# Three joints of a feed-forward layer: token forms in column parts, a second queue for the first down weights, a PSUM bank for each output half

## The chip, the cores and the metric

The kernel runs on one core of a Trainium2 chip. The metric is the device time of one execution in microseconds (us). The trace calls the engines PE (TensorE, matmuls), DVE (VectorE), ACT (ScalarE), POOL (GpSimd) and SP (SyncE, which here only starts DMAs; its queue is SPq). TensorE accumulates in PSUM, which has eight banks, each 512 fp32 columns wide on 128 partitions.

## What is computed

One layer of an encoder, for a prompt of 1024 tokens and a sample of 64, with model width 1024 and feed-forward width 2816. Ahead of the feed-forward lie three token-mixing branches, which the change does not touch. What matters here is the end:

```python
    x = x + rms_norm(merged @ w_out, g_mix_post)

    h2 = rms_norm(x, g_ffn_pre)
    up = h2 @ w_ffn_up
    up_full = jnp.concatenate([ffn_left.astype(up.dtype), up], axis=1)
    upc = causal_dwconv(up_full, ffn_dw_w)
    fg, fv = jnp.split(upc, 2, axis=-1)
    x = x + rms_norm((jax.nn.gelu(fg) * fv) @ w_ffn_down, g_ffn_post)
    return (x, k, v, u_full[:, -(CONV_WIDTH - 1):], up_full[:, -(FFN_CONV_WIDTH - 1):])
```

The last item returned, the last two rows of `up`, are the `ffn_state` outputs.

## The kernel before

All products are fp32 made of rounded parts: an operand is split (`split`, lines 99 and 100) into a high part (a cast on ACT) and a low part (a subtraction on DVE), and three products of parts are added in PSUM.

**Output projection** (1599.9 to 1700.9 us). Nine tiles of tokens, t = 0 to 8 (tile 8 is the sample). For each, 48 matmuls of `mgh`/`mgl` against the resident weights `woh`/`wol` into two banks (L1397 to L1400), 24 for each half e of the output columns. `finish` takes the tile's mean square (ACT, L1307), scales and adds the residual (DVE, L1312 and L1313, the sum kept in `xr` and stored to `d_x1`), takes the second mean square (L1316) and scales again into `tt` (L1318). Tiles are gathered in groups {0, 1}, {2, 3}, {4}, {5, 6}, {7}, {8}. `turn_group` queues eight pieces for each group: piece k transposes 128 features of the group's tokens on PE (L1330, tile `h2T<first tile>_<k>`) and an ACT copy with a gain puts them into `mf` (L1332). The pieces are taken from the list `turns` between the matmuls by `turn_some`, which keeps an estimated time `now` and lets a piece go every `gap`. After a group's last piece its list in `THEN` goes to `others`, which `turn_some` hands out every `rest`. So the program order on each engine is fixed by these estimates, when the program is written; nothing is reordered on the chip.

**Feed-forward up** (to 2194 us). For each of 22 feature blocks f, gate and value together are one 2 x 2 block product that is made with seven products j = 0 to 6 in place of eight. Each takes a sum or difference of token quarters (`X[g][j]`, tiles `xa<j>h`, `xa<j>l` for token columns up to 548, group A; `xb<j>h`, `xb<j>l` for group B) and one of weight blocks (`wf<j>`, made by `w_form` from the loaded `gw`, `vw`). A product of one group is 12 matmuls of 274 columns (L1452 to L1454) into a bank of `ff<f>_<j><g>`. Sums of token quarters are made in place by `sub` (L1237), the temporary ones in `wsl` and `wsh`, later in rows of `mf`. Group A's forms come from `forms_a`, whole (4 x 274 = 1096 columns at a time), after the group {4}. Group B's sums are made in three parts after {5, 6}, {7} and {8}; its forms are split whole once all transposes are done, ahead of block 0's products for group B. Block 0 runs its seven products for group A, with the last tiles' transposes between, then the seven for group B; from block 1 on a product serves both groups. The weight forms run five products ahead (`AHEAD`); those of block 1 are all made after the last product of block 0. Behind a product come the three-tap convolution (L1492, L1494), gelu (L1507), gate times value (L1511) and the store to `d_gu` (L1512).

**Down projection** (2208.5 us to the end). `wd_load` loads 128 rows of the weights (`wdr`, L1553) and splits them into `wd<f>h`, `wd<f>l`; `g_load` loads gate-value columns from `d_gu` (L1564, `g_0r`, `g_384r` and so on) and splits them. All loads stand on SP, in program order. Tiles 0 to 2 run together, f by f, each of their matmuls 512 columns wide (L1582, L1583, L1585). The other six tiles run one by one, the features in chunks of 6, 6, 6 and 4, in each chunk first all of output half 0, then all of half 1. After the last chunk of a half `close_half` takes the mean square (ACT, L1600; a copy on L1597 and a sum on L1598 go ahead of it for the sample) and multiplies by the gain (DVE, L1601) into `fo`. `y_banks` takes one tile of two banks from the pool `ff`, which feed-forward up used before, and gives each half one of them. Between the stages two transposes (`flT`) turn the last two rows for the `ffn_state` outputs.

## Time and profile before

| | us |
|---|---|
| median of 3 runs | 2488.18 |
| lowest, highest | 2487.49, 2489.12 |
| profiled execution, its time | 2489.66 |
| span of that profile | 2487.9 |
| TensorE busy in the span | 2409.8 (97%) |

The span reaches from the first to the last instruction of the profile; the execution's own time has 1.76 us more. All moments below count from the span's start. A row of a timeline has the start, the duration, the engine, the line, the operation, the names output<-inputs without their numbers, and in brackets the idle time of the engine just before and what ended it. Matmuls are pipelined: one that lasts 0.29 us can be followed by the next after 0.13. In a row of windows each engine has its busy time and, in brackets, its instructions; the last three numbers are the granted clock of TensorE as a share of full speed, the busy share of the DMA engines and GB/s.

### The profile page before, as it was taken

Reading aid. Unit: us, or ns where it says so; the run is one execution under the profiler, and the core shown is the slowest. Engines: PE = TensorE matmul, PEld = TensorE weight load, DVE = VectorE, ACT = ScalarE, POOL = GpSimd, SP = SyncE. Lnnn points to the kernel's source line nnn. Section 1 sums busy time; section 2 is a strip of 40 time slices with the busy share of each in tenths; the row PEclk is TensorE's granted clock in tenths of the full one; section 3 lists DMA queues with packets and bytes.
Section 4 is the critical chain, followed back from the end, with each engine's and each line's share of the span. In section 5 each row is a group of like instructions: output and inputs, shape, how many; then the busy total and the mean of one; then the engine's idle time right before and its main releaser. Section 6 shows DMA issues by size and latency. Waiting matters only on the chain.

```text
span 2487.9 us, 37659 instructions
## 1 busy us (share of the span) xinstructions
PE 2409.8 (97%) x15167; PEld 2280.5 (92%) x15167; DVE 1703.2 (68%) x2081; ACT 1055.2 (42%) x1965; POOL 103.4 (4%) x263
## 2 busy tenths in 40 slices
PE   8999999999999999999989999998999999979998
PEld 6999999999899998999889999986999999968776
DVE  6687878888665887787887436338988888853221
ACT  7324242424555666666664203145433333333111
POOL 2000000000000000000000000011101111100000
PEclk9999999999999999999999999998999999989999
DMA  7222222121555332433353546122222222155331
GB/s 266 89 66 87 75 67 93 62 93 62 155 158 135 86 89 74 100 90 92 95 162 124 196 139 203 59 94 68 79 79 79 79 70 78 46 160 160 101 95 41
DMA packets 287183, 257.74 MB, mean 104 GB/s; under 512 B 63407, under 2 KB 255555, under 8 KB 287009
## 3 DMA queue, kind: packets, MB, share of 16 engines
q1 hardware_dynamic: 287009, 255.34, 34.1%
q8 instruction: 119, 1.95, 0.3%
q14 instruction: 55, 0.45, 0.1%
HBM read 165.47 MB, written 68.19 MB: 94 GB/s over the span
## 4 chain that ended last, share of the span: by engine, by line
PE 54%; DVE 5%; issue 3%; ACT 2%; DMA 1%; POOL 1%; SPq 0%; ACTq 0%; DVEq 0%; POOLq 0%
PE ff L1452 6%; PE ff L1454 6%; PE ff L1453 6%; PE dn L1582 4%; PE dn L1583 4%; PE dn L1585 3%; PE aT L859 1%; PE cv L158 1%; PE sb L158 1%; PE sb L157 1%; PE cv L157 1%; PE cv L156 1%; PE sb L156 1%; DVE r L808 1%; PE av L878 1%
## 5 line engine op out<-in xcount | busy, mean ns | idle before, releaser
L423 DVE SCALAR_TENSOR_TENSOR acc<-u,cw,acc 128x1118 f32<-128x1118 f32 x240 | 331.6, 1382 | 5.6
L99 ACT CAST whi<-wraw 128x1024 fp32r<-128x1024 f32 x112 | 118.1, 1054 | 294.3 <-PE cv L157 73.1
L808 DVE TENSOR_TENSOR_SCAN r<-r 128x128 f32<-128x128 f32 (+7 forms) x128 | 173.3, 1355 | 65.4 <-ACT r L804 64.8
L156 PE MATMUL g<-hh,whi 128*128 128x362 f32 (+1 forms) x576 | 190.6, 331 | 0.0
L158 PE MATMUL g<-hh,wlo 128*128 128x362 f32 (+1 forms) x576 | 189.9, 330 | 0.0
L157 PE MATMUL g<-hl,whi 128*128 128x362 f32 (+1 forms) x576 | 189.8, 330 | 0.0
L100 DVE TENSOR_TENSOR wlo<-wraw,whi 128x1024 fp32r<-128x1024 f32 x112 | 136.5, 1220 | 35.3 <-ACT whi L99 35.2
L1464 DVE TENSOR_TENSOR mf<-mf,ff 128x548 f32<-128x548 f32 (+1 forms) x161 | 110.3, 697 | 57.8 <-PE ff L1454 57.6
L1494 DVE SCALAR_TENSOR_TENSOR mf<-mf,fw 128x1090 f32<-128x1090 f32 x88 | 118.9, 1351 | 16.0 <-ACT mf L1492 15.3
L100 DVE TENSOR_TENSOR atl<-aT,ath 128x512 fp32r<-128x512 f32 (+1 forms) x160 | 98.4, 631 | 26.4 <-ACT ath L99 25.4
L99 ACT CAST ath<-aT 128x512 fp32r<-128x512 f32 (+1 forms) x160 | 85.4, 550 | 68.0 <-PE aT L859 58.7
L803 ACT ACTIVATE be<-z 128x128 f32<-128x128 f32 (+2 forms) x192 | 95.6, 498 | 36.1 <-PE z L832 20.9
L156 PEld LDWEIGHTS g<-hh,whi 128*128 128x128 f32 x576 | 108.9, 189 | 0.1
L157 PEld LDWEIGHTS g<-hl,whi 128*128 128x128 f32 x576 | 108.5, 188 | 0.2
L158 PEld LDWEIGHTS g<-hh,wlo 128*128 128x128 f32 x576 | 108.4, 188 | 0.0
L809 DVE TENSOR_TENSOR be<-be,r 128x127 f32<-128x127 f32 (+7 forms) x128 | 96.6, 755 | 3.0
L804 ACT ACTIVATE r<-z 128x128 f32<-128x128 f32 (+2 forms) x192 | 95.8, 499 | 0.1
L877 PE MATMUL av<-ath,vp 128*128 128x256 f32 x320 | 82.2, 283 | 1.7 <-DVE os L884 1.3
L878 PE MATMUL av<-atl,vp 128*128 128x256 f32 x320 | 78.8, 285 | 1.9 <-DVE atl L100 1.9
L544 ACT ACTIVATE gt<-g 128x362 f32<-128x362 f32 (+1 forms) x72 | 33.8, 470 | 84.8 <-PE g L158 83.4
L830 PE MATMUL z<-ks,qd 128*128 128x256 f32 (+2 forms) x192 | 69.8, 365 | 0.0
L156 PE MATMUL v<-hh,whi 128*128 128x384 f32 (+1 forms) x192 | 69.4, 361 | 0.0
(1441 smaller groups left out, 7856.2 us busy)
## 6 DMA issues: line engine op xcount, KB each, us to landing
wraw<-in_w_in SPq DMA_DIRECT2D x72, 512.0 KB, 3.9
d_gate<-gt SPq DMA_DIRECT2D x24, 544.0 KB, 4.2
d_gu<-mf SPq DMA_DIRECT2D x22, 545.0 KB, 3.1
vw<-in_w_ffn_up SPq DMA_DIRECT2D x22, 512.0 KB, 3.7
gw<-in_w_ffn_up SPq DMA_DIRECT2D x22, 512.0 KB, 3.9
wdr<-in_w_ffn_down SPq DMA_DIRECT2D x22, 512.0 KB, 4.7
wraw<-in_w_mem_kv SPq DMA_DIRECT2D x16, 512.0 KB, 5.1
qd<-qd SPq DMA_DIRECT2D x24, 272.0 KB, 4.1
```

Of the source, the lines that this page charges most:

```text
L99: ACT.copy(out=hi, in_=src)
L100: DVE.tensor_tensor(out=lo, in0=src, in1=hi.bitcast(F32), op=ALU.subtract)
L156: PE.matmul(ps, wh[:, k, :], rh[k][c], start=first, stop=False)
L157: PE.matmul(ps, wh[:, k, :], rl[k][c], start=False, stop=False)
L158: PE.matmul(ps, wl[:, k, :], rh[k][c], start=False, stop=last)
L423: DVE.scalar_tensor_tensor(out=acc, in0=u[:, t : t + 1118], scalar=cw[:, t * 8 + i : t * 8 + i + 1], in1=acc, op0=ALU.mult, op1=ALU.add,)
L808: DVE.tensor_tensor_scan(out=rv, data0=rv, data1=rv, initial=1.0, op0=ALU.mult, op1=ALU.min)
L1452: PE.matmul(ps, w[:, k, :], xh[:, k, :], start=k == 0, stop=False)
L1453: PE.matmul(ps, w[:, k, :], xl[:, k, :], start=False, stop=False)
L1454: PE.matmul(ps, w[:, 4 + k, :], xh[:, k, :], start=False, stop=k == 3)
L1464: DVE.tensor_tensor(out=out, in0=a, in1=ps, op=ALU.add)
L1494: DVE.scalar_tensor_tensor(out=acc, in0=raw[:, t : NO + t], scalar=fw[:, t * 44 + m : t * 44 + m + 1], in1=acc, op0=ALU.mult, op1=ALU.add,)
```

## The change

There are five parts.

1. `forms_a` is replaced by `sums(g, j0, j1)`, which makes sums and splits for columns j0 to j1 of a quarter. Group A's are made in columns 0 to 238 after the group {2, 3} and in 238 to 274 after {4}. `turn_some` lets a piece go every 0.6 in place of 1.2 estimated us, and a queued form every 1.2 in place of 1.6.
2. Group B's splits are made in the same three column parts as its sums (74, 128, 72). They are kept and written out after the last piece, ahead of the second half of block 0; what of them can run earlier does so as the engines reach them.
3. Block 1's weight forms are made one by one behind products 1 to 5 of the second half of block 0.
4. `wdr0`, `wdr1` and the first gate-value tile are loaded by DMAs that ACT starts. The copy of `flT` goes to rows of `mf` that are free and stands, with the two state stores, ahead of the last store to `d_gu`. On SP the load of the gain `gfpost`, which stood behind the loads for features 2 to 6, comes right behind that store, ahead of the second gate-value tile.
5. The pool `ff` is closed after feed-forward up, and the down projection takes each output half from a pool `yp` of eight tiles of one bank.

```diff
-    def turn_some(dt, gap=1.2, rest=1.6):
+    def turn_some(dt, gap=0.6, rest=1.2):
...
-    def forms_a():
-
-        q11, q12, q21, q22 = quarters(0)
+    def tiles_a():
         X[0] = x_tiles(
...
+    def sums(g, j0, j1):
+
+        if g == 0 and X[0] is None:
+            tiles_a()
+        t2, t3 = (w[:, : 4 * NG].rearrange("p (k t) -> p k t", k=4) for w in ws) if g == 0 else (T2, T3)
+        q11, q12, q21, q22, t2, t3 = (q[:, :, j0:j1] for q in quarters(g) + [t2, t3])
 
         def form(j, src):
-            return lambda: split(*X[0][j], src)
-
-        return [
-            lambda: sub(t3, q22, q12), form(0, q11), lambda: sub(q12, q12, q11), lambda: sub(t2, q22, q12), form(1, t2),
-            form(2, t3), form(3, q12), form(4, q22), form(5, q21), lambda: sub(q21, q21, t2), form(6, q21),
+            return lambda: split(*(x[:, :, j0:j1] for x in X[g][j]), src)
+
+        return [lambda: sub(t3, q22, q12), lambda: sub(q12, q12, q11), lambda: sub(t2, q22, q12)], [
+            form(0, q11), form(1, t2), form(2, t3), form(3, q12), form(4, q22), form(5, q21),
+            lambda: sub(q21, q21, t2), form(6, q21),
         ]
...
+    PART = TP // 2 - NG
+    kept = []
 
     def sums_b(j0, j1):
-        q11, q12, q21, q22, t2, t3 = (q[:, :, j0:j1] for q in quarters(1) + [T2, T3])
-        return [lambda: sub(t3, q22, q12), lambda: sub(q12, q12, q11), lambda: sub(t2, q22, q12)]
-
-    LAST = (0, TP - 128 - 548 - NG, TP - 548 - NG, NG)
-    THEN = {4: forms_a, 5: lambda: sums_b(0, LAST[1]), 7: lambda: sums_b(*LAST[1:3]), 8: lambda: sums_b(*LAST[2:])}
+        first, then = sums(1, j0, j1)
+        kept.append(then)
+        return first
+
+    def sums_a(j0, j1):
+        first, then = sums(0, j0, j1)
+        return first[:1] + then[:1] + first[1:] + then[1:]
+
+    THEN = {
+        2: lambda: sums_a(0, PART), 4: lambda: sums_a(PART, NG),
+        5: lambda: sums_b(*LAST[0:2]), 7: lambda: sums_b(*LAST[1:3]), 8: lambda: sums_b(*LAST[2:4]),
+    }
...
-    ff = ctx.enter_context(tc.tile_pool(name="ff", bufs=4, space=PSUM, reuse_waits="tile"))
+    ff = banks.enter_context(tc.tile_pool(name="ff", bufs=4, space=PSUM, reuse_waits="tile"))
...
-    X[1] = x_tiles(lambda j, e: bp.tile([P, 4, NG], F32R, name=f"xb{j}{e}"))
-    q11, t1, q21, q22 = quarters(1)
-    for j, src in enumerate((q11, T2, T3, t1, q22, q21, q21)):
-        if j == 6:
-            sub(q21, q21, T2)
-        split(*X[1][j], src)
+    assert len(kept) == 3
+    for fs in kept:
+        for f in fs:
+            f()
     AHEAD = 5
     for j in range(7):
         product(0, j, (1,))
-        for n in range(AHEAD) if j == 6 else ():
-            w_form(1, n)
+        if 0 < j <= AHEAD:
+            w_form(1, j - 1)
...
+    fo = mf[:88, 7, 256 : 256 + 2 * P]
+    ACT.copy(out=fo, in_=tp[:88, : 2 * P])
+    for a, nm in enumerate(("ffn_state_prompt", "ffn_state_sample")):
+        SP.dma_start(out=O[nm][0, 0].rearrange("r (f c) -> (r f) c", c=P), in_=fo[:, a * P : (a + 1) * P])
     held.close()
+    banks.close()
+    yp = ctx.enter_context(tc.tile_pool(name="yp", bufs=8, space=PSUM, reuse_waits="tile"))
...
-            SP.dma_start(out=raw, in_=I["w_ffn_down"][0][f * P : (f + 1) * P, :])
+            (ACT if f < 2 else SP).dma_start(out=raw, in_=I["w_ffn_down"][0][f * P : (f + 1) * P, :])
...
-        SP.dma_start(
+        (ACT if f0 == t0 == 0 else SP).dma_start(
             out=raw.rearrange("p (f t) -> p f t", f=nf),
...
     def y_banks(t):
-        both = ff.tile([P, 2, 512], F32, tag="ff", name=f"dn{t}", bufs=4)
-        return [both[:, e, :] for e in range(2)]
+        return [yp.tile([P, 512], F32, tag="y", name=f"dn{t}_{e}", bufs=8) for e in range(2)]
```

What this does to the order of instructions is shown at three places. In these rows a name ends with a running number of its tile, and the brackets name the counters that the instruction waits for.

ScalarE beside output tile 6, before (`h2T2_k` and `h2T4_k` are transposed pieces of tiles 2, 3 and of tile 4, `tt5` the squares of tile 5, `mgh7` the next tile's high part):

```order
L1307 ACTIVATE tt5_16631,oms5_16632<-y5_0_16550 128x512 [waits PE_49,Pool_49]
L1332 ACTIVATE mf_14602<-h2T2_5_16595,vec_91 128x256 [waits PE_49]
L1332 ACTIVATE mf_14602<-h2T2_6_16605,vec_91 128x256 [waits PE_49]
L1332 ACTIVATE mf_14602<-h2T2_7_16615,vec_91 128x256 [waits PE_49]
L1332 ACTIVATE mf_14602<-h2T4_0_16625,vec_91 128x128 [waits PE_49]
L99 CAST mgh7_16649<-mf_14602 128x1024 [waits PE_49]
L1307 ACTIVATE tt5_16631,oms5_16632<-y5_1_16551 128x512 [waits PE_49]
L1332 ACTIVATE mf_14602<-h2T4_1_16660,vec_91 128x128 [waits PE_49]
L1332 ACTIVATE mf_14602<-h2T4_2_16669,vec_91 128x128 [waits PE_49]
L1332 ACTIVATE mf_14602<-h2T4_3_16678,vec_91 128x128 [waits PE_49]
```

The same place now:

```order
L1307 ACTIVATE tt5_16643,oms5_16644<-y5_0_16554 128x512 [waits PE_49,Pool_49]
L99 CAST xa1h_16452<-wsh_16464 128x4x238 [waits DVE_49]
L1332 ACTIVATE mf_14602<-h2T4_0_16632,vec_91 128x128 [waits PE_49]
L1332 ACTIVATE mf_14602<-h2T4_1_16638,vec_91 128x128 [waits PE_49]
L99 CAST xa2h_16454<-wsl_16465 128x4x238
L1307 ACTIVATE tt5_16643,oms5_16644<-y5_1_16555 128x512
L99 CAST mgh7_16661<-mf_14602 128x1024
L1332 ACTIVATE mf_14602<-h2T4_2_16672,vec_91 128x128 [waits PE_49]
L1332 ACTIVATE mf_14602<-h2T4_3_16678,vec_91 128x128 [waits PE_49]
```

The cast of group A's form 1 (`xa1h`, from the sum `wsh` that VectorE makes) stands ahead of the copies of tile 4's first two pieces, and further casts lie between the others.

VectorE ahead of block 0's products for group B, before (`xb0l` is the low part of group B's first form; the rows of 4 x 128 and 4 x 72 columns on L1237 are sums of token quarters, L1464 adds a product):

```order
L100 TENSOR_TENSOR xb0l_17128<-mf_14602,xb0h_17127 128x1096
L1464 TENSOR_TENSOR mf_14602<-mf_14602,ff0_40_17049 128x274 [waits DVE_49,PE_49]
L1237 TENSOR_TENSOR mf_14602<-mf_14602 128x4x128 [waits Activation_49]
L100 TENSOR_TENSOR xb5l_17138<-mf_14602,xb5h_17137 128x1096
L1237 TENSOR_TENSOR mf_14602<-mf_14602 128x4x128 [waits DVE_49]
L1464 TENSOR_TENSOR mf_14602<-mf_14602,ff0_50_17070 128x274 [waits PE_49]
L1237 TENSOR_TENSOR mf_14602<-mf_14602 128x4x128 [waits DVE_49]
L1464 TENSOR_TENSOR mf_14602<-mf_14602,ff0_60_17089 128x274 [waits PE_49]
L1237 TENSOR_TENSOR mf_14602<-mf_14602 128x4x72 [waits Activation_49]
```

The last rows ahead of the same form's last part now:

```order
L1237 TENSOR_TENSOR mf_14602<-mf_14602 128x4x72 [waits Activation_49]
L100 TENSOR_TENSOR xb1l_16994<-mf_14602,xb1h_16993 128x4x128 [waits Activation_49]
L1237 TENSOR_TENSOR mf_14602<-mf_14602 128x4x72 [waits DVE_49]
L100 TENSOR_TENSOR xb3l_16998<-mf_14602,xb3h_16997 128x4x128
L1237 TENSOR_TENSOR mf_14602<-mf_14602 128x4x72 [waits DVE_49]
L100 TENSOR_TENSOR xb4l_17000<-mf_14602,xb4h_16999 128x4x128
L100 TENSOR_TENSOR xb5l_17002<-mf_14602,xb5h_17001 128x4x128
L100 TENSOR_TENSOR xb0l_16992<-mf_14602,xb0h_16991 128x4x72
```

The low part of form 0 for the last 72 columns stands behind three sums of 72 and the splits of 128 columns of forms 1, 3, 4 and 5. In before form 0 was split whole, ahead of the sums of the last parts, which do not touch it.

TensorE where tile 3 of the down projection goes from output half 0 to half 1, in the last chunk, before (`dn3` holds both halves, `wd18h` and `g18_384h` are high parts of weights and gate-value):

```order
L1582 MATMUL dn3_22505<-wd21h_22374,g18_384h_22592 128x512
L1583 MATMUL dn3_22505<-wd21l_22375,g18_384h_22592 128x512
L1585 MATMUL dn3_22505<-wd21h_22374,g18_384l_22593 128x512
L1582 MATMUL dn3_22505<-wd18h_22296,g18_384h_22592 128x512 [waits DVE_49]
L1583 MATMUL dn3_22505<-wd18l_22297,g18_384h_22592 128x512
L1585 MATMUL dn3_22505<-wd18h_22296,g18_384l_22593 128x512
```

And now (`dn3_0` and `dn3_1` are the halves):

```order
L1601 MATMUL dn3_0_22559<-wd21h_22428,g18_384h_22647 128x512
L1602 MATMUL dn3_0_22559<-wd21l_22429,g18_384h_22647 128x512
L1604 MATMUL dn3_0_22559<-wd21h_22428,g18_384l_22648 128x512
L1601 MATMUL dn3_1_22560<-wd18h_22350,g18_384h_22647 128x512
L1602 MATMUL dn3_1_22560<-wd18l_22351,g18_384h_22647 128x512
L1604 MATMUL dn3_1_22560<-wd18h_22350,g18_384l_22648 128x512
```

The first matmul of half 1 waited for VectorE and carries no wait now. The other five tiles that run one by one show the same.

## Rows read from the trace of the kernel before

**Rows 1.** The page, busy time, share of the span and instructions of TensorE

```profile
PE 2409.8 (97%) x15167; PEld 2280.5 (92%) x15167; DVE 1703.2 (68%) x2081; ACT 1055.2 (42%) x1965; POOL 103.4 (4%) x263
```

**Rows 2.** Windows: busy us (instructions) of each engine, granted clock, DMA

```profile
1599.90:1700.90 101.00, 101.00 (x469) 82.26 (x468) 47.85 (x51) 44.26 (x91) 17.28 (x39) 1.00 0.21 71
1700.90:1727.50 26.60, 18.97 (x105) 16.85 (x104) 21.82 (x35) 16.42 (x38) 3.19 (x7) 0.74 0.37 109
1727.50:1747.00 19.50, 14.74 (x95) 14.21 (x95) 17.22 (x26) 10.93 (x16) 2.08 (x6) 0.82 0.00 1
1747.00:2194.00 447.00, 447.00 (x3520) 447.00 (x3519) 374.00 (x474) 171.35 (x226) 49.33 (x126) 1.00 0.22 72
2194.00:2208.50 14.50, 0.44 (x5) 0.18 (x3) 7.78 (x8) 4.45 (x5) 0.00 (x0) 0.59 0.48 156
2221.00:2300.00 79.00, 79.00 (x351) 65.40 (x350) 30.90 (x29) 26.00 (x30) 0.00 (x0) 1.00 0.57 171
2300.00:2487.90 187.90, 172.46 (x753) 140.47 (x751) 43.02 (x52) 28.92 (x59) 9.06 (x18) 1.00 0.27 78
```

**Rows 3.** Timeline of TensorE, 1700 to 1750: start, us, what, [idle before]

```profile
1703.39 0.39 PE L1452 MATMUL ff<-xa0h,wf 128*128 128x274 f32 x1 [2.31 <-ACT mf L1332]
...
1709.41 0.59 PE L1452 MATMUL ff<-xa1h,wf 128*128 128x274 f32 x1 [2.70 <-ACT wf L99]
...
1712.46 0.60 PE L1454 MATMUL ff<-xa1h,wf 128*128 128x274 f32 x1 [2.23 <-DVE wf L100]
...
1732.43 0.60 PE L1452 MATMUL ff<-xb1h,wf 128*128 128x274 f32 x1 [3.14 <-ACT xb1h L99]
...
1734.65 0.60 PE L1453 MATMUL ff<-xb1l,wf 128*128 128x274 f32 x1 [1.62 <-DVE xb1l L100]
...
1745.76 0.29 PE L1452 MATMUL ff<-xa0h,wf 128*128 128x274 f32 x1
```

**Rows 4.** Groups of VectorE by form, 1599.9 to 1750: busy, mean ns

```profile
L1237 DVE TENSOR_TENSOR wsh<-mf 128x1096 f32<-128x1096 f32 x1 | 1.3, 1296 | 0.0
...
L1237 DVE TENSOR_TENSOR mf<-mf 128x288 f32<-128x288 f32 x3 | 1.4, 456 | 1.0 <-ACT mf L1332 1.0
...
L100 DVE TENSOR_TENSOR wf<-gw,wf 128x512 fp32r<-128x512 f32 x4 | 2.7, 682 | 0.0
```

**Rows 5.** Timeline of VectorE, 1663 to 1673

```profile
1664.84 0.75 DVE L1318 TENSOR_SCALAR tt<-xr,or 128x1024 f32<-128x1024 f32 x1 [2.24 <-POOL or L198]
```

**Rows 6.** Timelines of ScalarE, SP's queue and TensorE, 2193 to 2216

```profile
2195.29 1.21 ACT L1492 ACTIVATE mf<-mf,fw 128x1090 f32<-128x1090 f32 x1 [2.06 <-DVE mf L1464]
2196.56 1.12 ACT L1507 ACTIVATE mf<-mf 128x1090 f32<-128x1090 f32 x1
...
2200.70 0.32 SPq L1512 DMA_DIRECT2D d_gu<-mf  x1
2201.12 0.37 SPq L1553 DMA_DIRECT2D wdr<-in_w_ffn_down  x1
2201.59 0.82 SPq L1564 DMA_DIRECT2D g_0r<-d_gu  x1
...
2205.81 1.05 ACT L99 CAST wd0h<-wdr 128x1024 fp32r<-128x1024 f32 x1 [7.88 <-DMA wdr<-in_w_ffn_down]
2207.60 0.83 ACT L99 CAST g_0h<-g_0r 128x768 fp32r<-128x768 f32 x1 [0.75 <-DMA g_0r<-d_gu]
...
2208.49 0.79 PE L1582 MATMUL dn<-wd0h,g_0h 128*128 128x512 f32 x1 [14.06 <-ACT g_0h L99]
...
2215.16 0.39 PE L1582 MATMUL dn<-wd1h,g_0h 128*128 128x512 f32 x1
```

**Rows 7.** DMA engines from 2190 to 2201.5

```profile
DMA packets 2, 0.02 MB, mean 2 GB/s; under 512 B 0, under 2 KB 0, under 8 KB 0
```

**Rows 8.** TensorE waits, 2290 to 2488: total, times, longest; one place

```profile
PE dn L1582 <- DVE fo L1601: 7.8, 5, 1.6
PE dn L1582 <- DVE fo L1598: 1.4, 1, 1.4
...
2327.83 0.39 PE L1585 MATMUL dn<-wd21h,g_384l 128*128 128x512 f32 x1
...
2329.72 0.50 PE L1582 MATMUL dn<-wd18h,g_384h 128*128 128x512 f32 x1 [1.50 <-DVE fo L1601]
```

More of the change, by code (lines that the diff above doesn't have):

```diff
@@ L1517, in encoder_step @@
     w_load(1)
+    X[1] = x_tiles(lambda j, e: bp.tile([P, 4, NG], F32R, name=f"xb{j}{e}"))
     for j in range(7):
@@ L1631, in encoder_step @@
     junk = gp.tile([P, 512], BF16, name="junk")
-    fo = gp.tile([88, 2 * P], F32, name="flo")
-    ACT.copy(out=fo, in_=tp[:88, : 2 * P])
-    for a, nm in enumerate(("ffn_state_prompt", "ffn_state_sample")):
-        SP.dma_start(out=O[nm][0, 0].rearrange("r (f c) -> (r f) c", c=P), in_=fo[:, a * P : (a + 1) * P])
     ys = {t: y_banks(t) for t in first}
```

2 lines of the change are left out of this document (1 added, 1 removed).

## The prediction

> **What bounds the kernel now.** I read the page's busy shares first, then the mean clock and busy time by stage, then TensorE's own rows in the stages where it is not full, and last what it waited for there. TensorE is busy 97% of the span [rows 1], so only a stage where it is not full has something to give. By stage [rows 2] it is full in the output projection (101.00 of 101.00 us), in the feed-forward from the second feature block on (447.00 of 447.00) and in the down projection's first part (79.00 of 79.00). It is not full at three joints, and those are what the change touches.
>
> Joint 1, from 1700.9 (last product of the output projection) to 1745.76 (first matmul of feature block 1) [rows 2, 3]: 44.86 us. The work in it is 14 products of 12 matmuls. 3520 matmuls in 447.00 us [rows 2] is 0.127 us each, so 14 x 12 x 0.127 = 21.3 us. Some sixteen transposes of the last token tiles come on top; no row has one alone, so I bound one between 0.06 us (0.127 x 128/274, by columns) and 0.25, take 0.14, and have 2.3 us (1.0 to 4.0). So 23.6 us is work and 21.3 us is loss. Of that loss 2.31 + 2.70 + 2.23 + 3.14 + 1.62 = 12.0 us are five waits that name their releasers [rows 3]: the copy of a transpose, the weight forms, the halves of group B's token forms. The other 9.3 us is clock: the two stretches ran at 0.74 and 0.82 of full [rows 2], between the levels 1.2 and 2.4 GHz, and a matmul takes 0.60 us there against 0.29 [rows 3].
>
> Joint 2, 2194 to 2208.5: TensorE busy 0.44 of 14.50 us [rows 2]. The first down matmul waited 14.06 us for the cast of the first gate tile [rows 6]. Behind it is a chain: the last gate-value store leaves SP at 2200.70, and only behind it in SP's queue go the first down weights (2201.12) and the first gate tile (2201.59), which neither need nor touch that store's data.
>
> Joint 3, the rest of the down projection: 172.46 of 187.90 busy [rows 2]. Of this, six waits of TensorE for VectorE, 7.8 + 1.4 = 9.2 us [rows 8], are of one kind: the second output half's first matmul of the last feature chunk waits until VectorE has read the first half. Both halves are one tile of two banks.
>
> **The change part by part.**
>
> *Own bank for each half.* It removes those six waits: the second half's matmul carries no wait now. Price of one: the last matmul of half 0 starts at 2327.83, the next would start 0.23 later (2328.06), it starts at 2329.72 [rows 8]: 1.66 us, and about 0.1 us more because it lasts 0.50 and not 0.39. With 5 x 1.75 for the longer kind and 1.64 for the other: 10.4 us (at least 9.2, by the waits alone). What is late next there? ScalarE's and VectorE's pass over half 0 now lies beside 12 matmuls of half 1 (2.8 us), against 1.4 us that it takes. The clock stays 1.00 in this stage, so nothing else comes back. The tail after the last matmul is what it was. I take 10.4, range 9.2 to 10.8.
>
> *Down weights and first gate tile on ScalarE's queue.* They no longer stand behind the store. ScalarE is free for them after the last gelu (2196.56 + 1.12 = 2197.68); the copy of the state rows is moved ahead of the gelu, into 2.06 us that ScalarE waits there anyway [rows 6], so it costs nothing as long as that wait stands, else its 0.35 us. So the weights go at about 2197.75 in place of 2201.12, the gate tile at about 2198.2 in place of 2201.59. From issue to cast the gate tile took 2207.60 - 2201.59 = 6.0 us and the cast 0.83 [rows 6]: 2198.2 + 6.0 + 0.83 = 2205.0, against 2208.49. No load leaves ScalarE's queue in the trace of before; SP's issues here last 0.32 to 0.82 us [rows 6]. If each of the two ahead takes 0.82, the start is 2206.2 and the gain 2.3; if the gate tile lands in the 4.7 us of the weights, 2203.7 and 4.8. Less than nothing would need a ScalarE that is held past 2201.12, and nothing stands on it then. Moved along: the two small state stores now go ahead of the last gate-value store, when SP is idle; the 0.5 MB gain load now stands on SP ahead of the second gate tile. ScalarE casts in order, so the second weights' cast stands behind that second gate tile: issued near 2201.6, landing some 6 us later, cast by 2208.4, the weights' halves by 2210.7, and feature block 1 needs them 2215.16 - 2208.49 = 6.7 us after the first matmul [rows 6], at 2211.7. Margin 1.0 us; beyond it, each us late is a us of TensorE. I take 3.5 us (1.3 to 4.8, the lower end with a us of such lateness).
>
> Here a rule speaks against the change. The rows show the loads held 3.4 us by an unrelated wait at the head of SP's queue [rows 6]. The Trainium skill (DMA: Bandwidth & Descriptors, section "Issuing engines are not separate DMA queues") says that loads started on several engines run on the same 16 DMA engines and save only the sequencer's time to initiate them. By it the part would be worth some 0.8 us, the sum 15.3 and the time 2472.9. In this place what is saved is a wait at the queue's head, which the rule does not speak of; no run here shows a load on ScalarE's queue.
>
> *Token forms.* Group A's forms are made in 238 and 36 columns, the first part already beside output tiles 5 and 6; group B's in 74, 128 and 72 columns beside the first half of block 0; block 1's weight forms go among the second half's products. The work is the same number of elements and some 30 more instructions; VectorE (47.85 of 101.00 us) and ScalarE (44.26) have room in total [rows 2]. The order in which they stand decides. I followed the four engines' queues through joint 1 with the trace's duration of each kind; [rows 4] has the three that the lines below use (a pass of 952 columns, by 1.30 us for 1096, is 1.13, and 1.2 with its start).
>
> - Tile 6: VectorE comes free of tile 4 at 1664.84 + 0.75 [rows 5] and then runs four passes of 1.2 and a small one: the sum that ScalarE's cast of form 1 needs is ready at about 1670.8. Behind that cast stand the copies of transposes 4_0 and 4_1 on ScalarE, and transposes 4_2 and later need their two banks. TensorE, which waited for nothing here, waits 1.7 + 1.3 us, with 0.35 in tiles 3 and 5: 3.35 us. A bound below is 0, if the sums run earlier.
> - Tile 8: ScalarE's first weight cast waits for a load that itself waits for a store of tile 6's rows; transpose 5_3 stands behind it: 1.54 us. Block 0 then begins after the last copy of group {5, 6}: 1.45 us, where the wait was 2.31.
> - First half of block 0: 1.55 (a copy late in ScalarE's order), 1.77 (transpose 7_2 behind a weight cast) and 0.5: 3.8 us, against 2.70 + 2.23 and slow clock.
> - Second half: its second matmul needs form 0's low part for the last 72 columns. After the last copy stand on VectorE three sums of 72 columns (0.46 each), four splits of 128 (0.68 each) and then this split (0.46): 4.6 us, against 3.14 + 1.62. I add 2.5 us of half-speed matmuls behind it.
>
> The loss is 3.35 + 1.54 + 1.45 + 3.8 + 4.6 + 2.5 = 17.2 us, in place of 21.3: a gain of 4.1 us; block 1 would start at about 1741.7. From block 1 on TensorE found every form ready and I find no new wait.
>
> *Sum.* 10.4 + 3.5 + 4.1 = 18.0 us. The profiled execution took 2489.66 us, its span 2487.9 plus 1.76 around it; less 18.0 that is 2471.7. The median of the three runs, 2488.18, is 1.5 below the profiled execution, so 2470.2.
>
> **The rivals.**
>
> *Joint 1 as meant* (0.27): sums and casts run early enough that tiles 3 to 8 stay full, and the clock stays up through block 0. For it: 53 us of VectorE's and 57 us of ScalarE's time in the output projection are free [rows 2]. Against: in-order queues at the places above. Without the first two lines and the added slow clock, 17.2 - 4.9 - 2.5 = 9.8 us of loss remain, so joint 1 gives 11.5, the sum is 25.4 and the time 2462.8.
>
> *Joint 1 gives nothing* (0.20): the stalls of tile 6 and of the first half each bring TensorE to the lower level, as the waits of 2 to 3 us did in before. Two more such half-speed stretches cost 2.5 us each: joint 1 loses 0.9, the sum is 13.0 and the time 2475.2.
>
> *Slower* (0.02): the wait of tile 6 recurs in each of the groups {4}, {5, 6}, {7} and {8}, each time at 2.5 us and with the whole clock loss of joint 1 as it was in before (9.3 us), 11.8 together: 47 us in place of 21.3, 26 us more against 13.9 from the other joints: 2500. It decides from 35.2 us of loss in joint 1 on, three recurrences. Against it: these groups' copies are spread over 12 us each.
>
> *The bank split does nothing* (0.03): if the second half is held by something that ends as late as VectorE's read, joint 3 gives 0: sum 7.6, time 2480.6. Against: the chain has nothing else there.
>
> *Only issue time is saved at joint 2* (0.05), the mechanism in which the loads, though issued earlier, land little earlier, because they wait for the same transfers: then only the issues ahead of the gate tile are saved, 0.32 for the store and 0.47 for the weights [rows 6], 0.8 us in place of 3.5. Sum 15.3, time 2472.9. Against: the DMA engines moved 0.02 MB in the 11.5 us up to the store [rows 7].
>
> **How the numbers follow.** The forecast has 0.43, its own range 2467 to 2473. About 0.2% (5 us) is what a measurement of this kernel can tell from no change. Leaving out a tenth at either end, the range is 2461 to 2479. Faster by over 0.2% means below 2483.2: all cases but the slower one and part of the split's, 0.95; within it 0.03; slower 0.02.
>
> **What would show it.** Right: no wait of `dn` matmuls for the line that reads half 0, and a stage of 177.5 us where it was 187.9; the first weights issued on ScalarE's queue within 0.3 us of the gelu's end and the first `dn` matmul near 3.5 us earlier after the last feed-forward matmul; transposes of tile 4 waiting on ScalarE in tile 6, and a wait of 4 to 5 us at the second matmul of block 0's second half. Wrong: output tiles with no wait at all and block 1 starting 33 us after the last output matmul (joint 1 as meant), or granted clock under 1.00 between tiles 5 and 8 (nothing gained there).

## The result and the profile after

The changed kernel takes 2474.55 us (median of 4 runs, 2470.70 to 2475.29) against 2487.91 for the kernel before on the same chip (median of 4). The ratio is 0.9942, 95% interval 0.9925 to 0.9960: about 13.4 us faster, with 18.0 forecast. The profiled execution took 2475.29 us, its span is 2473.5.

To see where the time went, I read a few moments from TensorE's timeline in each profile and took the lengths between them. "Joint 1" here runs from the first matmul of the output projection to the first of feature block 1, so that it also holds what the output tiles lose. "Joint 2" is from the last feed-forward matmul to the first matmul of down block 2, "blocks 2 to 21" from there to the first matmul of tile 3, "joint 3" from there to the last matmul of all.

| us | before | after | difference | forecast |
|---|---|---|---|---|
| joint 1 | 145.87 | 143.86 | -2.0 | -4.1 |
| rest of the feed-forward | 448.15 | 448.15 | 0 | 0 |
| joint 2 | 25.34 | 23.83 | -1.5 | -3.5 |
| blocks 2 to 21 | 81.60 | 81.85 | +0.25 | 0 |
| joint 3 | 180.39 | 169.32 | -11.1 | -10.4 |
| tail | 6.66 | 6.69 | 0 | 0 |

The differences give 14.3 of the 14.4 us by which the spans differ; the rest lies ahead of joint 1. Joint 3 came as forecast; each of the other two gave about half.

TensorE's share on the page is 97% again (busy time 2408.1 us, as in [rows 1] within 2 us): the work is the same, less of the span is empty. The windows by stage, with the columns of [rows 2] (span and busy time of each engine with its instructions, then granted clock, DMA share and GB/s), of the changed kernel:

```profile
1599.90:1705.30 105.40, 101.87 (x473) 82.16 (x471) 55.43 (x71) 48.24 (x106) 17.45 (x40) 1.00 0.20 71
1705.30:1743.60 38.30, 29.54 (x185) 27.43 (x185) 33.39 (x67) 23.48 (x58) 4.78 (x12) 0.87 0.24 68
1743.60:2191.90 448.30, 448.30 (x3530) 448.30 (x3530) 374.47 (x474) 172.46 (x227) 49.76 (x126) 1.00 0.22 72
2191.90:2200.20 8.30, 0.42 (x4) 0.17 (x2) 7.30 (x7) 4.50 (x5) 0.00 (x0) 0.80 0.60 196
2200.20:2215.60 15.40, 12.22 (x36) 8.86 (x37) 4.62 (x5) 3.49 (x4) 0.00 (x0) 0.78 0.78 243
2215.60:2297.40 81.80, 81.80 (x361) 67.44 (x361) 34.56 (x33) 29.81 (x38) 1.00 (x3) 1.00 0.56 171
2297.40:2473.50 176.10, 169.79 (x750) 140.25 (x748) 41.18 (x50) 26.62 (x53) 10.23 (x16) 0.99 0.29 84
```

What to see: the output projection, full in [rows 2], is 105.40 long and 3.5 us of it are empty. The empty stretch ahead of the first down matmul shrank from 14.50 to 8.30. But the first two down blocks that follow, full once they had begun in before, have 3.2 us of waits (their granted clock is 0.78; over the same two blocks of before it was 0.76).

TensorE's timeline in joint 1 (start, length, instruction, idle time before it and what ended it), changed kernel, answering to [rows 3]:

```profile
1671.16 0.33 PE L1330 MATMUL h2T<-ident,tt 128*128 128x128 f32 x1 [1.13 <-ACT mf L1332]
...
1674.09 0.33 PE L1330 MATMUL h2T<-ident,tt 128*128 128x128 f32 x1 [1.09 <-ACT mf L1332]
...
1698.30 0.44 PE L1330 MATMUL h2T<-ident,tt 128*128 128x128 f32 x2 [1.22 <-ACT mf L1332]
...
1706.30 0.40 PE L1466 MATMUL ff<-xa0h,wf 128*128 128x274 f32 x1 [0.82 <-ACT mf L1332]
...
1711.59 0.39 PE L1466 MATMUL ff<-xa2h,wf 128*128 128x274 f32 x1 [1.73 <-ACT mf L1482]
...
1713.83 0.33 PE L1330 MATMUL h2T<-ident,tt 128*128 128x128 f32 x1 [1.21 <-ACT mf L1332]
...
1730.52 0.60 PE L1467 MATMUL ff<-xb0l,wf 128*128 128x274 f32 x1 [4.37 <-DVE xb0l L100]
...
1743.66 0.29 PE L1466 MATMUL ff<-xa0h,wf 128*128 128x274 f32 x1
```

The waits for weight forms of [rows 3] are gone. In their place stand those that the orders of ScalarE and VectorE named: the two of tile 4's transposes in output tile 6, one in tile 8, two in the first half of block 0, and the long one at the second matmul of its second half. At the start of block 0 a wait of 0.82 us stands where it was 2.31.

Joint 2, rows of ScalarE, of the two DMA queues (ACTq, SPq) and of TensorE, answering to [rows 6]:

```profile
2194.46 1.11 ACT L1521 ACTIVATE mf<-mf 128x1090 f32<-128x1090 f32 x1
2194.46 0.39 ACTq L1572 DMA_DIRECT2D wdr<-in_w_ffn_down  x1
2194.89 0.44 ACTq L1583 DMA_DIRECT2D g_0r<-d_gu  x1
...
2198.35 1.04 ACT L99 CAST wd0h<-wdr 128x1024 fp32r<-128x1024 f32 x1 [2.78 <-DMA wdr<-in_w_ffn_down]
2199.33 0.83 ACT L99 CAST g_0h<-g_0r 128x768 fp32r<-128x768 f32 x1
...
2198.60 0.35 SPq L1526 DMA_DIRECT2D d_gu<-mf  x1
2199.04 0.38 SPq L1656 DMA_DIRECT2D gfpost<-in_g_ffn_post  x1
2199.51 0.79 SPq L1583 DMA_DIRECT2D g_0r<-d_gu  x1
...
2206.97 0.83 ACT L99 CAST g_0h<-g_0r 128x768 fp32r<-128x768 f32 x1 [6.80 <-DMA g_0r<-d_gu]
2207.70 1.04 ACT L99 CAST wd1h<-wdr 128x1024 fp32r<-128x1024 f32 x1
...
2200.22 0.80 PE L1601 MATMUL dn<-wd0h,g_0h 128*128 128x512 f32 x1 [7.89 <-ACT g_0h L99]
...
2208.80 0.50 PE L1601 MATMUL dn<-wd1h,g_0h 128*128 128x512 f32 x1 [2.33 <-ACT wd1h L99]
2210.06 0.50 PE L1602 MATMUL dn<-wd1l,g_0h 128*128 128x512 f32 x1 [0.76 <-DVE wd1l L100]
```

The first down matmul comes 8.41 us after the last feed-forward matmul (2191.81), where it was 14.58: a gain of 6.2, more than the 3.5 forecast. It does not last. The second weights' cast (`wd1h`) stands on ScalarE behind the second gate tile's. That tile's load was issued on SP behind the store and the 0.5 MB gain load, and its cast began 7.5 us later. ScalarE idled 6.80 us in front of it, and TensorE then waited 2.33 + 0.76 us at block 1.

Joint 3: in [rows 8] six waits, 9.2 us; from 2215 us on the changed kernel's TensorE has no wait at all. The place of [rows 8] where tile 3 goes from half 0 to half 1, now 0.23 us from one matmul to the next:

```profile
2324.46 0.39 PE L1604 MATMUL dn<-wd21h,g_384l 128*128 128x512 f32 x1
2324.69 0.39 PE L1601 MATMUL dn<-wd18h,g_384h 128*128 128x512 f32 x1
```

### The profile page after: what moved, and what is told of

Its sections match the earlier page's. It is cut to its first block, busy times and chain, and to the rows that moved or that the text cites. A ratio compares the mean times of both kernels' runs of the same rounds, so it can differ in the third digit from the quotient of the medians.

```text
span 2473.5 us, 37712 instructions
## 1 busy us (share of the span) xinstructions
PE 2408.1 (97%) x15167; PEld 2279.3 (92%) x15167; DVE 1705.1 (69%) x2108; ACT 1055.2 (43%) x1986; POOL 105.6 (4%) x263
## 4 chain that ended last, share of the span: by engine, by line
PE 54%; DVE 5%; ACT 2%; issue 2%; DMA 1%; POOL 1%; SPq 0%; DVEq 0%; POOLq 0%; ACTq 0%
PE ff L1466 6%; PE ff L1467 6%; PE ff L1468 6%; PE dn L1602 4%; PE dn L1601 4%; PE dn L1604 3%; PE aT L859 1%; DVE r L808 1%; PE cv L158 1%; PE sb L158 1%; PE sb L157 1%; PE cv L157 1%; PE cv L156 1%; PE sb L156 1%; PE av L878 1%
## 5 line engine op out<-in xcount | busy, mean ns | idle before, releaser
L1508 DVE SCALAR_TENSOR_TENSOR mf<-mf,fw 128x1090 f32<-128x1090 f32 x88 | 118.9, 1352 | 16.8 <-ACT mf L1506 16.1
```

The source lines that it names most:

```text
L1508: DVE.scalar_tensor_tensor(out=acc, in0=raw[:, t : NO + t], scalar=fw[:, t * 44 + m : t * 44 + m + 1], in1=acc, op0=ALU.mult, op1=ALU.add,)
```

## The experiments

Eleven variants and the kernel before again. The table has the lengths as above, in us, for each profile; the text below says what was changed. The last column is the median time, with the kernel before at 2487.0 to 2489.4 beside them.

| kernel | joint 1 | joint 2 | blocks 2 to 21 | joint 3 | time |
|---|---|---|---|---|---|
| before | 145.87 | 25.34 | 81.60 | 180.39 | 2487.91 |
| before again | 145.27 | 25.87 | 81.60 | 180.37 | 2487.93 |
| banks only | 144.27 | 25.04 | 83.15 | 169.32 | 2478.98 |
| queue only | 143.90 | 18.64 | 84.32 | 180.42 | 2484.77 |
| forms only | 143.71 | 24.57 | 81.60 | 180.40 | 2486.21 |
| after | 143.86 | 23.83 | 81.85 | 169.32 | 2474.55 |
| second gate tile on ScalarE's queue | 143.97 | 18.57 | 83.82 | 169.32 | 2471.58 |
| the same, three raw buffers | 142.38 | 18.74 | 86.27 | 169.32 | 2471.12 |
| splits by form | 139.20 | 22.02 | 83.68 | 169.32 | 2469.16 |
| old pace | 139.75 | 23.98 | 82.17 | 169.32 | 2469.10 |
| group A whole | 144.27 | 22.01 | 85.01 | 169.32 | 2475.73 |
| three mends | 139.31 | 19.04 | 81.60 | 169.32 | 2465.15 |
| three mends, slow pace | 135.90 | 18.85 | 81.60 | 169.31 | 2461.52 |
| three mends, middle pace | 136.72 | 18.88 | 81.60 | 169.32 | 2462.51 |

**One part at a time.** First theory: the three joints are separate, and the parts add up.

Banks only, on the kernel before:

```diff
-    ff = ctx.enter_context(tc.tile_pool(name="ff", bufs=4, space=PSUM, reuse_waits="tile"))
+    ff = banks.enter_context(tc.tile_pool(name="ff", bufs=4, space=PSUM, reuse_waits="tile"))
...
     held.close()
+    banks.close()
+    yp = ctx.enter_context(tc.tile_pool(name="yp", bufs=8, space=PSUM, reuse_waits="tile"))
...
-        both = ff.tile([P, 2, 512], F32, tag="ff", name=f"dn{t}", bufs=4)
-        return [both[:, e, :] for e in range(2)]
+        return [yp.tile([P, 512], F32, tag="y", name=f"dn{t}_{e}", bufs=8) for e in range(2)]
...
```

> The kernel before with the bank of its own for each output half alone (and what it needs: the state copy and its stores go ahead of the last gate-value store, and the feed-forward's pool is closed). Theory, joints are separate and the six waits are all of joint 3: the down projection's one-by-one part is 10.4 to 11.1 us shorter, the joints ahead of it stay as in the kernel before, time 2476.8 to 2477.6. Rival, part of the changed kernel's 11.1 us at that joint comes from its earlier start or its other loads: under 9.2 us, time above 2478.7.

Measured 2478.98 us (2475.71 to 2481.34; ratio 0.9958, 0.9943 to 0.9973), just above the rival's bound of 2478.7. But joint 3 itself is 169.32 in this kernel, 11.1 us shorter, to the hundredth the length it has in the changed kernel. Of that, 1.55 us came back in blocks 2 to 21: TensorE's timeline there has two waits at block 16, for a gate tile's cast and for its low part, which the kernel before does not have:

```profile
2275.88 0.50 PE L1588 MATMUL dn<-wd16h,g_0h 128*128 128x512 f32 x1 [0.30 <-ACT g_0h L99]
2277.28 0.50 PE L1591 MATMUL dn<-wd16h,g_0l 128*128 128x512 f32 x1 [0.66 <-DVE g_0l L100]
```

So the six waits are all of joint 3 and worth 11.1 us. That the gate tiles come late is another matter, taken up below.

Queue only, on the kernel before:

```diff
-            SP.dma_start(out=raw, in_=I["w_ffn_down"][0][f * P : (f + 1) * P, :])
+            (ACT if f < 2 else SP).dma_start(out=raw, in_=I["w_ffn_down"][0][f * P : (f + 1) * P, :])
...
-        SP.dma_start(
+        (ACT if f0 == t0 == 0 else SP).dma_start(
```

> The kernel before with the first two down weights and the first gate tile loaded from ScalarE's queue, alone. Here the order on ScalarE puts the second weights' cast ahead of the second gate tile's, and on SP the gain load still stands ahead of the second gate tile. Theory, in the changed kernel the block-1 wait of 2.3 + 0.8 us comes from the order of the two casts on ScalarE: no such wait here, the first down matmul 6 us earlier than before and block 2 some 5 to 6 us earlier, time 2482 to 2483. Rival, the loads from two queues share the DMA engines and the second weights land late whatever the order: a wait of 2 to 3 us at block 1 again, a gain of 1.5, time 2486.4.

Measured 2484.77 us (2483.87 to 2488.51; ratio 0.9987, 0.9977 to 0.9996), 4 us less than before on that chip (2488.88), where the theory had 2482 to 2483. Joint 2 went from 25.34 to 18.64, 6.7 us, with no wait at block 1; then blocks 2 to 21 took 2.7 us more, which the theory did not have. Rows of ScalarE, SP's queue and TensorE show both, in the queue-only kernel:

```profile
2201.57 1.05 ACT L99 CAST wd1h<-wdr 128x1024 fp32r<-128x1024 f32 x1 [0.27 <-DMA wdr<-in_w_ffn_down]
2207.59 0.83 ACT L99 CAST g_0h<-g_0r 128x768 fp32r<-128x768 f32 x1 [4.97 <-DMA g_0r<-d_gu]
...
2243.60 0.38 SPq L1564 DMA_DIRECT2D g_0r<-d_gu  x1
...
2259.40 1.05 ACT L99 CAST wd18h<-wdr 128x1024 fp32r<-128x1024 f32 x1 [2.81 <-DMA wdr<-in_w_ffn_down]
2260.35 0.83 ACT L99 CAST g_0h<-g_0r 128x768 fp32r<-128x768 f32 x1
...
2261.23 0.50 PE L1582 MATMUL dn<-wd14h,g_0h 128*128 128x512 f32 x1 [0.50 <-ACT g_0h L99]
2262.62 0.50 PE L1585 MATMUL dn<-wd14h,g_0l 128*128 128x512 f32 x1 [0.66 <-DVE g_0l L100]
```

Here the second weights are cast as soon as they land, at 2201.57, and the late gate tile stands behind them and is in time for block 2. The order of the two casts was the cause of the block-1 wait, not a late load of the weights. The second group of rows is the giving back: at block 14 TensorE waits for a gate tile whose cast stands behind that of weights 18, which are needed four blocks later and were waiting for their load. The gate tile's own load had been issued at 2243.60, 16.8 us ahead of its cast, while the gate tiles of joint 2 took at most 7.5 from issue to cast.

Forms only is the changed kernel with the loads, banks and state stores of before:

> The kernel before with the token forms' column parts, the faster pace of the transposes and block 1's weight forms moved, alone; loads and banks as before. Theory, the joints add up: block 1 starts 2.1 us earlier as in the changed kernel, with the same waits (tile 6 two of 1.1, block 0's second half 4.4), time 2485.8. Rival, the shared profile hides more (the forecast's 4.1): 2483.8.

Measured 2486.21 us (2482.89 to 2487.85; ratio 0.9988, 0.9978 to 0.9998). Joint 1 is 143.71, with the same waits (1.13, 1.10, 1.75, 4.37). The theory fits; but what to compare it with is in doubt, since the two other kernels, in which every engine's instructions up to block 1 stand in the order of before, show 144.27 and 143.90 and not 145.87. To answer that, the kernel before was run once more, unchanged:

> The kernel before once more, for a second profile of its first joint. In its profile block 1 starts 145.9 us after the first output matmul; in the kernels that change only the banks or only the queue, with the same code up to there, 144.3 and 143.9. Theory, the stretches at the lower clock fall differently from execution to execution, and the joint takes 144 to 146 us here too: then the changed kernel's gain there is between 0 and 2 us. Rival, 145.9 is fixed for this kernel and something in the other two shortens it: 145.7 to 146.1 again.

It took 2487.93 us (one run), and joint 1 was 145.27: not the 145.87 that the rival called fixed. The same 16 us of the program, from 104.11 us after the first output matmul, in the two executions of the kernel before, first the one of [rows 2 and 3], then this one (columns as above; the clock is the third number from the end):

```profile
1704.00:1720.00 16.00, 11.06 (x54) 10.41 (x55) 12.98 (x21) 10.49 (x22) 2.40 (x5) 0.57 0.38 105
```

```profile
1702.37:1718.37 16.00, 10.36 (x65) 9.81 (x66) 13.80 (x24) 10.85 (x23) 2.39 (x5) 0.79 0.39 103
```

One execution passed 54 instructions at 0.57 and the other 65 at 0.79, with the same waits but for one (2.70 and 3.41 us for the weight form). Two stretches tell the four executions of this joint apart. Granted clock, with the stretch counted from the first output matmul:

| kernel | 104.1 to 120.1 us | 131.5 to 139.0 us | joint 1, us |
|---|---|---|---|
| before | 0.57 | 0.56 | 145.87 |
| before again | 0.79 | 0.58 | 145.27 |
| banks only | 0.79 | 0.77 | 144.27 |
| queue only | 0.79 | 0.77 | 143.90 |

So the stretches at the lower of the two levels (1.2 and 2.4 GHz) fall differently under the same order of instructions, as the theory has it. The profiles are not all from one chip, so whether the chip has a part in it is not shown.

Four executions of the old joint 1 took 143.9 to 145.9, mean 144.8; four of the new one (after, forms only, and the two variants of joint 2 with the second gate tile) 142.4 to 144.0, mean 143.5. The forms' part is worth some 1.3 us, not surely distinguishable from nothing by the profiles alone; the timed runs of forms only put it at 0.5 to 5.5 us, with a joint 2 that is 0.8 us shorter in its profile.

**The giving back at joint 2.** Second theory: order of casts on ScalarE. Changed kernel, one edit:

```diff
-        (ACT if f0 == t0 == 0 else SP).dma_start(
+        (ACT if t0 == 0 and f0 <= 2 else SP).dma_start(
```

> The changed kernel, with the second gate tile also loaded from ScalarE's queue, right behind the first one's cast, which puts its cast behind the second weights' on ScalarE. Theory, order of casts: no wait at block 1, the 3.1 us and some 1.5 us of half-speed matmuls behind it go, time 2470. Rival, shared transfers: the wait stays near 3 us, time 2474.5.

Measured 2471.58 us (2470.42 to 2472.54). Joint 2 is 18.57, 5.3 us less than in the changed kernel, with no wait at block 1; 2.0 of it came back in blocks 2 to 21 (waits of 0.67 and 0.30 for gate tiles at blocks 14 and 16, with slower matmuls beside them, 0.50 us where others last 0.39). The rival, that the weights land late whatever the order, is out.

Are the gate tiles late because the weights' loads have only two raw buffers, or because weights are placed ahead of them? The same kernel with `bufs=3` for the raw tiles `wdr` and `x1_`:

> The changed kernel with the second gate tile on ScalarE's queue, and three raw buffers for the down weights in place of two. ScalarE's order then has five weight casts ahead of the gate tiles that are needed sooner (the tile of features 10 behind weights 17). Theory, the waits of 0.7 and 0.3 us at features 14 and 16 that gave back 2 us come from gate tiles standing behind weights in ScalarE's order, not from too few raw buffers: they stay or grow, block 2 to tile 3 takes 83.8 us or more, time 2471.5 or more. Rival, the weights' stream is held by its two buffers: the waits go, 81.6 us, time 2469.5.

Measured 2471.12 us, but blocks 2 to 21 took 86.27: the giving back, against the 81.60 of before, grew from 2.2 to 4.7 us (a shorter joint 1 in this execution hides it in the time). ScalarE's and TensorE's rows with three raw buffers:

```profile
2239.82 1.05 ACT L99 CAST wd17h<-wdr 128x1024 fp32r<-128x1024 f32 x1 [1.20 <-DMA wdr<-in_w_ffn_down]
2240.78 0.83 ACT L99 CAST g_0h<-g_0r 128x768 fp32r<-128x768 f32 x1
...
2241.66 0.50 PE L1601 MATMUL dn<-wd10h,g_0h 128*128 128x512 f32 x1 [0.94 <-ACT g_0h L99]
```

The order on each engine is laid out when the program is built, and with another buffer the weights are placed further ahead: the gate tile of block 10 stands behind weights 17, seven blocks on. Its load had been issued at 2223.33, 17.4 us ahead of its cast. So more buffers do not help, and what holds the gate tile is its place among the casts.

**Joint 1.** Theory: its waits are places in the orders of VectorE and ScalarE, not missing data. Changed kernel, the kept splits form by form:

```diff
-    for fs in kept:
+    for fs in zip(*kept):
         for f in fs:
             f()
```

> The changed kernel, with group B's kept splits written out form by form (all three column parts of form 0, then of form 1, and so on) in place of part by part. On VectorE form 0's last 72 columns then stand before the last sums; form 1's last part still stands behind them. Theory, the 4.4 us wait at block 0's second half is a place in VectorE's order and not a lack of data: the second matmul of the half no longer waits, a wait of 1.5 to 2.5 us remains at form 1, block 1 starts 143.9 - 2.5 = 141.4 us after the first output matmul, time 2472. Rival, the last sums' data set the end: the waits of the half stay 4 us in sum, block 1 at 143.9, time 2474.5.

Measured 2469.16 us (2467.44 to 2470.13), 5.4 less than the changed kernel; joint 1 fell by 4.7 to 139.20, where the theory had 141.4. TensorE at the start of the second half:

```profile
1727.15 0.39 PE L1466 MATMUL ff<-xb1h,wf 128*128 128x274 f32 x1 [1.62 <-ACT xb1h L99]
1727.79 0.40 PE L1467 MATMUL ff<-xb1l,wf 128*128 128x274 f32 x1 [0.25 <-DVE xb1l L100]
```

The 4.37 us wait became 1.62 + 0.25, 2.5 less, and the matmul behind the wait lasts 0.39 us in place of 0.60. The windows from the first matmul behind the wait to block 1, first of the changed kernel, then of this one:

```profile
1730.50:1743.66 13.16, 13.14 (x83) 13.14 (x84) 12.26 (x26) 5.25 (x10) 2.07 (x6) 0.79 0.01 2
```

```profile
1727.15:1738.44 11.29, 11.04 (x72) 10.83 (x73) 9.78 (x22) 3.78 (x7) 1.68 (x6) 0.85 0.01 2
```

From its first matmul to block 1 the second half is 3.2 us shorter (14.7 in place of 17.9): the 2.5 of waits and 0.7 at the higher clock, 0.85 in place of 0.79. The other 1.5 us fell in the first half, where executions of the changed order differ by as much among themselves (its end lies 124.2 to 126.1 us after the first output matmul in four of them, and at 124.5 here); that it belongs to this edit is not shown.

The kernel before's pace for transposes and forms, on the changed kernel:

```diff
-    def turn_some(dt, gap=0.6, rest=1.2):
+    def turn_some(dt, gap=1.2, rest=1.6):
```

> The changed kernel with the kernel before's pace: pieces of transposes every 1.2 and queued forms every 1.6 estimated us. On ScalarE the cast of form 1's first part then stands behind the copies of tile 4's first four pieces. Theory, the two waits of 1.1 us in output tile 6 come from that cast standing ahead of the copies: they go, the output tiles take 101 to 103 us in place of 105.3; what of it reaches block 1's start depends on the pieces that now lie later, 0 to 2.5 us earlier than 143.9, time 2472 to 2474.5. Rival, VectorE and ScalarE are too full there whatever the order: 105 us again.

At this pace two of group A's forms get their last 36 columns only after the weight sums have taken over the room of the token sums, so they hold other values and this kernel does not compute the layer; the instructions are the same, in another order, and it serves for its lengths alone. Measured 2469.10 us, below the 2472 to 2474.5 of the theory. The output tiles take 101.4 us in place of 105.3: on ScalarE the cast of form 1 now stands behind the copies of tile 4's first four pieces, and the two waits in tile 6 and the one in tile 8 are gone. All of it reached block 1: joint 1 139.75.

Group A's forms whole, after tile 4:

```diff
-        2: lambda: sums_a(0, PART), 4: lambda: sums_a(PART, NG),
+        4: lambda: sums_a(0, NG),
```

> The changed kernel with group A's forms made whole after the group of tile 4, as in the kernel before, the rest as changed. Theory, the column parts of group A bring the start of block 0 nothing that lasts, since block 0 waits for the last copies of tiles 5 and 6 and for weight forms: output tiles 101 us, block 1's start within 1.5 us of 143.9, time 2474.5. Rival, the early first part is what keeps block 0 fed: waits for weight forms of 2 to 3 us come back and block 1 starts 2 or more us later, time 2477.

Measured 2475.73 us (2474.51 to 2477.36), joint 1 144.27. The waits in output tile 6 are gone, as the theory has it, but not the loss. TensorE's waits from 1595 to 1760 (total, times, longest):

```profile
PE ff L1467 <- DVE xb0l L100: 5.5, 1, 5.5
PE h2T L1330 <- DVE tt L1318: 4.2, 1, 4.2
PE ff L1466 <- ACT mf L1482: 1.9, 1, 1.9
```

At the pace of 0.6 the first transpose of {5, 6} stands early in TensorE's order, and tile 6's scaled rows (`tt`) wait on VectorE behind the whole passes: 4.2 us in one piece. The theory's 101 us for the output tiles was wrong (106.9); its start of block 1 was right, 0.4 us from the 143.9, and the rival's waits for weight forms did not come back. So the fast pace costs waits in the output tiles with the column parts (1.13 + 1.09) and without them (4.17). The parts at a slower pace cost none in tile 6, in the run before this one and in the last two below.

**Together.** The three mends are the splits by form, the second gate tile on ScalarE's queue, and the order of loads and casts from feature 2 on held as written (which also puts the 0.5 MB gain load back to feature 12):

```diff
-    for f in range(NF):
-        wd_load(f + 3)
+    for FS in (range(2), range(2, NF)):
+        with tc.manual_schedule(engines={mybir.EngineType.SP, mybir.EngineType.Activation}) if FS[0] else ExitStack():
+            for f in FS:
+                wd_load(f + 3)
...
```

> The changed kernel with three mends: group B's splits form by form, the second gate tile on ScalarE's queue, and from feature 2 on the loads and casts of the first three tiles' down projection kept in the order in which they are written (weights f+3, f+3+1, then the gate tile f+4), on SP and ScalarE. Theory: order of casts was all that gave back joint 2's gain, so no wait of TensorE after the first down matmul, 18.6 us from the last feed-forward matmul to block 2 and 81.6 us on to tile 3; block 1 of the feed-forward 139 to 141 us after the first output matmul. Time 2474.5 - 4 - 5 = 2464 to 2466. Rival, the loads themselves are late: waits of 1 to 2 us stay between blocks 2 and 21 and the time is 2467 or more.

Measured 2465.15 us (2464.16 to 2465.97; ratio to before 0.9904, 0.9889 to 0.9918). TensorE has one wait from 2185 to 2460, the first:

```profile
PE dn L1601 <- ACT g_0h L99: 7.9, 1, 7.9
```

Blocks 2 to 21 take 81.60 again, joint 2 19.04: joint 2 now gives 6.3 us and keeps them. The gate tiles' casts now stand ahead of the weights that come after them, while on SP their loads stand later than in the variant with the second gate tile alone (that of block 14 behind weights 15, there ahead of them). So the casts' order on ScalarE, and not the loads, had given the gain back.

The same with the slow pace, and with the middle one (`gap=0.9, rest=1.2`); in both, what is left of group A's forms is written out ahead of block 0:

> The same three mends with the kernel before's pace for transposes and forms (1.2 and 1.6), and whatever of group A's forms is still queued written out ahead of block 0, so that every form is made before it is read. Theory, the pace of 0.6 and 1.2 only brings waits into the output tiles: output tiles 101 us in place of 105.3, block 1 at 137 to 139 after the first output matmul, time 2462 to 2464. Rival, what lies later then stalls block 0 by as much: 139 to 141 and 2465.

> As the run with the slow pace, at 0.9 and 1.2. Theory, the cast of form 1's first part stands behind the copies of tile 4's first four pieces here too, so the output tiles lose at most 1 us, and fewer pieces are left for block 0 than at the slow pace: block 1 at 136 to 139, time 2461 to 2464. Rival, as there: 139 to 141 and 2465.

The slow pace took 2461.52 us. Its expectation that every form is made before it is read did not hold: what was left stands behind the weight sums, the same two forms hold other values as above, and its time counts for its order alone. In the middle pace all forms are made in time; it took 2462.51 us (2460.59 to 2463.29; ratio to before 0.9892, 0.9877 to 0.9907). Of the kernels here that compute the layer it is the fastest, 26 us under the kernel before and 12 under the changed one. Its output tiles take 102.4 us and joint 1 136.7, with no wait in tile 6.

## Why the prediction was right, and where its sizes were off

The direction and the range (2461 to 2479) held, and the banks came as the largest term; which of the other two is larger can't be told (1.5 and 1.3 to 2.0 us). The forecast was 4.4 us too low. In the other two terms errors of opposite sign hide part of each other, as told below; that the total missed by no more than this owes something to them.

*Bank for each half*: right in mechanism and nearly in size, 11.1 in place of 10.4, a little above its own range of 9.2 to 10.8. The step from one wait to six took 0.1 us for the restart behind a wait; the runs show 1.85 us for each of the six on average, 0.1 more.

*Loads on ScalarE's queue*: the 1.5 us lies in the stated range (1.3 to 4.8), but the sum of 3.5 was wrong on both sides. It let the loads go after the gelu's end; the rows show the DMA issue at 2194.46, with the gelu's start, 1.1 us sooner, and the loads took 3.9 and at most 4.4 us from issue to cast in place of 4.7 and 6.0. So the first matmul gained 6.2. Then the step that failed was "Margin 1.0 us": it was reckoned from a first matmul 2205.0 - 2193.91 = 11.1 us after the feed-forward. It came at 8.4 us, so block 1 was due 2.7 us sooner; and the second gate tile's cast began 15.2 us after the last feed-forward matmul, 1.5 later than the 13.7 (2207.6) that the prediction had. That makes 1.0 - 2.7 - 1.5 = 3.2 us too late, and 3.1 us were waited. The mechanism it named, the second weights behind that gate tile on ScalarE, was the right one; with the waits came a stretch of half-speed matmuls in block 1 (0.63 us where they last 0.39), some 2 us, which it had not priced. That left 1.5 of joint 2. A margin has to be moved along with the term that it guards: an earlier first matmul eats it.

The rival "only issue time is saved" is out: 6.2 us, not 0.8. The rule of the Trainium skill (DMA: Bandwidth & Descriptors, "Issuing engines are not separate DMA queues") does not fit this place, since what the second queue saved was SP's wait for the store's data. Its other half, one set of DMA engines for both, agrees with the second gate tile: from issue to cast it took 7.5 us on SP's queue, and no less on ScalarE's, 7.4 (2198.15 to 2205.52 in the variant with the second gate tile there), as long as the gain load went beside it; in the three mends, without the gain load, it took 5.4 (2195.07 to 2200.44).

*Token forms*: 4.1 forecast, 2.0 between the two profiles, 1.3 in the mean over four executions of each. The places of the waits were right, but for tiles 3 and 5, which had none:

| wait | forecast | measured |
|---|---|---|
| output tile 6, with tiles 3 and 5 | 3.35 | 2.2 |
| tile 8 | 1.54 | 1.2 |
| start of block 0 | 1.45 | 0.8 |
| first half | 3.8 | 1.73 + 1.21 + 0.34 + 0.28 = 3.6 |
| second half | 4.6 | 4.4 |
| lower clock and restarts | 2.5 | 7.1 (the rest) |

The last is the term that was mis-sized. Joint 1 is 143.86 long, of which 101.0 and 23.6 are work by the prediction's own count: 19.3 us of loss, 12.2 in waits and 7.1 in clock and restarts. Before, it was 21.3: 12.3 in waits (the five of [rows 3] and one of 0.28) and 9.0. So TensorE waits as long as it did, only at other places; the 2.0 us that were gained are clock and restarts, by which executions of one order differ too.

"I add 2.5 us of half-speed matmuls behind it" set a price on the clock for the second half alone. There it holds: 83 matmuls took 13.16 us at a granted clock of 0.79 (the window shown with the splits by form), and at 0.127 each they would take 10.5, so 2.6 went there. What the prediction put at nothing is the first half:

```profile
1705.40:1730.50 25.10, 16.36 (x102) 14.35 (x101) 21.19 (x42) 18.20 (x48) 2.62 (x6) 0.91 0.35 101
```

Of these 25.1 us 8.75 are waits and some 13.1 work (with the prediction's 2.3 for the transposes, which it bounds at 1.0 to 4.0), so some 3.3 are left, an estimate, at a granted clock of 0.91. Another 1.2 us stand in the output tiles, at 1.00, beside the waits there. That the loss of 17.2 was missed by only 2.1 is in part luck: the waits came out 2.5 us shorter in sum than forecast (12.2 in place of 14.7). And the before side of the sum rested on one execution at 145.87, the longest of four.

The case "joint 1 gives nothing" (0.20) has the nearest time, 2475.2, but not by its mechanism as a whole: the waits of tile 6 did not bring TensorE to the lower level, and the joint gave 1.3 to 2.0 us, between this case's -0.9 and the forecast's 4.1.

The slower case did not come: waits for copies like that of tile 6 came again in tile 8 and in block 0, but at 1.2 and not 2.5 us each and with the granted clock at 1.00 through the output tiles.

## What to carry to other kernels

When an edit moves loads or passes earlier, follow the in-order queue of every engine to the next instruction that stands behind them, and reckon each margin from the new, earlier due time: here a gain of 6.2 us left 1.5 because one cast stood in front of another, and a reordering without any new resource brought it back. A wait that is not for missing data but for a place in an order can be mended by writing the parts in the order in which they are used, and another buffer can make it worse. Two halves that are closed one after the other should not share one tile.

## What was not expected of the hardware

A DMA that stands behind an activation on ScalarE's queue was issued as that activation began (both at 2194.46 us), not after its 1.11 us. The same code at the same place ran at a granted clock of 0.57 in one execution and 0.79 in another over 16 us, and at 0.56 to 0.77 over a later 7.5 us; with it the joint moved by up to 2 us, so a term of this size can't be read from one profile. What sets which stretch falls to the lower level was not tried.
